# Inverse roots of the gating stage's norms: from ScalarE's tables to an integer step and three Newton steps on VectorE

## The chip, the cores and the metric

The kernel runs on one core of a Trainium2 chip. The metric is the device time of one execution in microseconds. The kernel before takes 2104.78 us, the median of three runs (2103.8 to 2104.8).

## The reference

One inference step of a two-layer encoder, for a prompt of 1024 rows and a sample of 32 rows that share weights, with 1024 channels. Layer 0 mixes by spatial gating, layer 1 by pooling; each layer has a squared-ReLU channel MLP of width 4096. RMS norms stand before and after each of them:

```python
def rmsnorm(x, g):
    y = x * lax.rsqrt(jnp.mean(x * x, axis=-1, keepdims=True) + EPS)
    return y * g

def sgu_mixer(h, w_in, g_v, w_s, b_s, w_out, T):
    z = jax.nn.gelu(h @ w_in)            # 1024 -> 4096
    u, v = jnp.split(z, 2, axis=-1)
    v = rmsnorm(v, g_v)                  # mean over 2048 values
    ...                                  # s = w_s v + b_s in chunks of 128 rows
    return (u * s) @ w_out, v

# trunk, one layer
x = x + gt1 * rmsnorm(mix, g_norm[i, 1])
h = rmsnorm(x, g_norm[i, 2]) * (1 + sc2) + sh2
f = jnp.square(jax.nn.relu(h @ ffn_w_up[i])) @ ffn_w_down[i]
x = x + gt2 * rmsnorm(f, g_norm[i, 3])
```

The change concerns how `lax.rsqrt` is computed for some of these norms.

## The kernel before

The 1056 rows are columns of three tiles: tile 0 and tile 1 have 384 prompt columns, tile 2 has 256 prompt and 32 sample columns. Channels lie on the partitions, in eight blocks (`KB`). Every product is made of three fp32r products: a matrix is split into a high and a low part (`wh`, `wl` for weights, `hh`, `hl` for inputs, `fh`, `fl` or `ush`, `usl` for hidden values). The high part is a copy on ScalarE (ACT), the low part a subtraction on VectorE (DVE); the matmuls run on TensorE (PE).

The gating layer goes through these stages. First the values `v` of all rows (the tile `pv`, `v_mm`, `v_end`): Gelu on ACT, a Square with accumulated sum, a store of `v`. `v_rms(t)` turns the sums of three row blocks into inverse roots `rv`, once per tile (L1283 on); the copies `wr` of the spatial weights are scaled with them. Then the items of `mixes`, two groups of 256 gate channels each: up products (`pu`), Gelu to `u`, the spatial product (`psp`), the gate, and the down products (`po`), whose sums lie in `acc`. Tile 0 goes first, then a pair stage for tiles 0 and 1 with combined inputs (`upairs`, `pgu`), then tile 2, then tiles 1 and 2. `sgu_stack.close()` ends the stage. After it come the MLP's up products `pf` and down products `pg`, first of tile 0, then of tile 1, then of both as a pair on combinations of the inputs (`combo`).

A norm over the channels is a `Stat`: ACT squares the blocks, DVE adds them, the sum is split (`sc` on ACT, `sm` on DVE), and two matmuls with ones (L977) give the sum `pn` in every partition. `Stat.finish` then takes the inverse root by `Abs_reciprocal_sqrt` on ACT (L981) and improves it by one Newton step: a Square on ACT (L982) and two scalar_tensor_tensors on DVE. `residual` multiplies by it and adds the old `x`, and starts the next `Stat`; `apply` makes `hh` and `hl` of the next product's input. In the profile the names carry the norm: `r_h` tile 2's input norm, `r_rs` the norm behind the gating, `r_r_0x` and `r_r_1x` the norms of tiles 0 and 1 in front of the MLP.

What an engine executes next is set in two steps. The program's own loop does it first: `weave` is called behind each product and pulls steps of the weight stream and of `fillers` (generators such as a tile's residual, or `u_sums`), as long as a planned DVE time is behind a planned PE time; `tick`, `tt`, `stt` and `ts` keep these times, and a filler that yields a number is not pulled again until the planned PE time has gone on by as much. Then the compiler's scheduler may still reorder. Each engine's queue is in order. A helper records every DVE operation, so these have one line, L80, in the profile. Weights come in through three raw buffers, with DMAs issued on SP.

`gelu` doesn't exist before the change; which norms run in the gating stage follows from the order of fillers: tile 2's input norm, tile 0's two norms behind the gating, and tile 1's first one.

Of the kernel before, what the change touches and what calls it, by code (L numbers as in the profile page):

```python
# [11 lines left out]
AF = mybir.ActivationFunctionType  # L12
ALU = mybir.AluOpType
# [3 lines left out]
D = 1024  # L17
# [18 lines left out]
def tile_stream_encoder_step(  # L36
# [25 lines left out]
    nc = tc.nc  # L62
    act = nc.scalar.activation
# [6 lines left out]
    def tick(us):  # L70
        time["pe"] += us
        time["dve"] = max(time["dve"], time["pe"] - 4.0)

    def on_dve(op, fixed, rate):
        def run(out, *args, **kw):
            n = 1
            for k in out.shape[1:]:
                n *= k
            time["dve"] += fixed + n / rate
            return op(out, *args, **kw)  # L80

        return run

    tt = on_dve(nc.vector.tensor_tensor, 0.07, 950.0)
    stt = on_dve(nc.vector.scalar_tensor_tensor, 0.13, 950.0)
    ts = on_dve(nc.vector.tensor_scalar, 0.13, 1900.0)
    turn32 = on_dve(nc.vector.transpose, 0.06, 880.0)

    def pool(name, **kw):
        return ctx.enter_context(tc.tile_pool(name=name, bufs=1, reuse_waits="tile", **kw))  # L90
# [15 lines left out]
    def acc_tile(t):  # L106
# [19 lines left out]
        out=quad, in_=ident.rearrange("p (c m) -> p m c", m=32), op=ALU.add, axis=AX.X  # L126
# [23 lines left out]
    def ps_ms(name):  # L150
        return psum.tile([P, 512], F32, tag="pm", bufs=3, name=name)

    def t_m(name):
        return work.tile([P, 384], F32, tag="m", bufs=3, name=name)
# [709 lines left out]
    def finish(tag):  # L864
        while any(f[0] == tag for f in fillers):
            pull(True)
        time["pe"] = max(time["pe"], time["dve"] - 3.0)


    def spread(t, ss, tag, out, dg):  # L870
# [18 lines left out]
        out.append(pb)  # L889
        yield False  # L890

    class Stat:


# [77 lines left out]
        def finish(self, out):  # L972
            n = self.n
            yield 1.2
            pn = ps_ms(f"pn_{self.tag}")
            for i, x in enumerate(self.parts):
                mm(pn[:, :n], onesr, x[:, :n], start=i == 0, stop=i == 1)  # L977
            tick(0.4)
            q = t_m(f"q_{self.tag}")[:, :n]
            r = work.tile([P, 384], F32, tag="rr", bufs=2, name=f"r_{self.tag}")[:, :n]  # L980
            act(out=r, in_=pn[:, :n], func=AF.Abs_reciprocal_sqrt, scale=1.0 / D)  # L981
            act(out=q, in_=r, func=AF.Square)  # L982
            yield 2.5
            stt(out=q, in0=pn[:, :n], scalar=-0.5 / D, in1=q, op0=ALU.mult, op1=ALU.mult)
            stt(out=r, in0=q, scalar=1.5, in1=r, op0=ALU.add, op1=ALU.mult)
            out.append(r)
            yield False


    def residual(st, l, cf, tag, out, store=True, stat=True, loads=None, r=None, small=False):  # L990
        t = st.t
        n = ncol[t]
        xos = {}

        def load(k2):
            xos[k2] = t_x(f"xo_{tag}_{k2}", [P, 2, n])
            i = nc.sync.dma_start(xos[k2], xd[t][:, 2 * k2 : 2 * k2 + 2, :])
            if loads is not None:
                loads.append(i.ins)

        if r is None:
            got = []
            yield from st.finish(got)
            r = got[0]
        st2 = Stat(t, tag + "x", small=small)
        for half in range(2):
            for k2 in (2 * half, 2 * half + 1):
                load(k2)
            for k2 in (2 * half, 2 * half + 1):
                for k in (2 * k2, 2 * k2 + 1):  # L1010
                    for c0, w, v in segs[t]:
                        a = A(t, k, c0, w)
                        stt(
                            out=a,
                            in0=a,
                            scalar=coef[:, l, cf, v, k : k + 1],
                            in1=r[:, c0 : c0 + w],
                            op0=ALU.mult,
                            op1=ALU.mult,
                        )  # L1020
                    yield True
                a = acc[t][:, 2 * k2 : 2 * k2 + 2, HALO:]
                tt(out=a, in0=a, in1=xos[k2], op=ALU.add)
                if stat:
                    st2.square(2 * k2, a)
                yield k2 % 2 == 0
        if store:
            nc.sync.dma_start(xd[t], acc[t][:, :, HALO:])
        out.append(st2)
# [253 lines left out]
    def v_rms(t):  # L1283
        c = slice(3 * t, 3 * t + 3)
        x, m, q = rv[:, c], rms[:, c, 0], rms[:, c, 1]
        nc.vector.tensor_reduce(out=x, in_=ssqv[:, c, :], op=ALU.add, axis=AX.X)
        ts(m, x, 1.0 / SGU, EPS, op0=ALU.mult, op1=ALU.add)
        act(out=x, in_=m, func=AF.Sqrt)
        nc.vector.reciprocal(out=x, in_=x)
        tt(out=q, in0=x, in1=x, op=ALU.mult)  # L1290
        stt(out=q, in0=q, scalar=-0.5, in1=m, op0=ALU.mult, op1=ALU.mult)
        stt(out=x, in0=q, scalar=1.5, in1=x, op0=ALU.add, op1=ALU.mult)

    hs = []

# [81 lines left out]
    for p, b in v_order:  # L1377
        ps = ps_dn(f"pv{p}_{b}")
        v_mm(ps, p, b, range(KB))
        v_end(ps, p, b)  # L1380
        next(h2_steps, None)
        if p == 2 and b < NT:
            with tc.issue_after(loads[("v", 2, 3)]):
                nc.sync.dma_start(xd[b], acc[b][:, :, HALO:])
        if p == 2 and b == NT - 1:
            u_open.append("acc")
        if p == 3 and b == 8:
            u_open.append("hs")
        if p == 3 and b % 3 == 2:
            v_rms(b // 3)  # L1390
        weave()
# [290 lines left out]
    def pair_item(p, after, ends, gate=None):  # L1682
# [59 lines left out]
        def up(jp):  # L1742
# [10 lines left out]
            if jp == 0:  # L1753
                flush()
                finish("combos" if gate is None else "usums")
                if state["kept"]:
                    state["kept"] = 0
                    for i in range(2):
                        x = w_tile(f"fu{i}", ("fu", i))
                        u_places.append((x[:, :n], x[:, n : 2 * n]))  # L1760
# [64 lines left out]
        if passes[p + 1][2] != PAIR:  # L1825
            slack[0] = 0.0
            finish(f"ffn{l}_{NT - 1}")
            fillers.append(late_norm.pop())
# [170 lines left out]
    for p, (gs, tiles) in enumerate(mixes):  # L1999
# [3 lines left out]
        for t in tiles:  # L2003
            sgu_item(p, t, mix, to_ffn0 if gs[-1] == 7 and t > 0 else None)

    sgu_stack.close()
    late = pool("late")

# [165 lines left out]
    def run_ffn(l, after):  # L2174
        for p, (pl, c, tiles, m) in enumerate(passes):
            if pl != l:
                continue
            ends = [t for t in tiles if not any(q[0] == l and t in q[2] for q in passes[p + 1 :])]
            if tiles == PAIR:
                pair_item(p, after, ends)  # L2180
                continue
            for t in tiles:
                if c == 0:
                    if any(f[0] == f"ffn{l}_{t}" for f in fillers):
                        flush()
                    finish(f"ffn{l}_{t}")
                ffn_item(p, t, after if t in ends else None)
# [158 lines left out]
```

## Time and profile before

| | us |
|---|---|
| median of three runs | 2104.78 |
| the profiled execution | 2107.3 |
| its span | 2105.5 |
| PE busy | 2078.7 |
| DVE busy | 1637.3 |
| ACT busy | 1069.1 |

The span is from the first instruction of the program to the last one; the profiled execution has 1.8 us around it. Rows of a timeline give the start in us, the duration in us, engine, line, operation, out<-in by the program's names, shapes, how many were merged, and in brackets the idle time of the engine just before and what ended it. ACT_TABLE_LOAD is ScalarE's change of its table of functions. The page says of itself that matmuls are pipelined and that their ends are modelled.

### The profile page before, as it was taken

How to read it: one execution, taken by the hardware profiler on the slowest of the kernel's cores; microseconds unless marked ns; L12 is line 12 of the kernel's file. 1: busy time of each engine (PE TensorE's matmuls, PEld its weight loads, DVE VectorE, ACT ScalarE, POOL GpSimd, SP SyncE). 2: the span in 40 equal slices, each digit the busy share in tenths (PEclk: the TensorE clock that was granted, in tenths of full speed). 3: DMA queues.
4: the chain of work that ended last, by engine and by line, in shares of the span. 5: the costliest groups of instructions: out<-in, count | busy, mean ns of one | idle time of the engine just before them, and what ended most of it. 6: DMA issues, size and time to landing. Idle time of an engine off the chain costs nothing.

```text
span 2105.5 us, 32900 instructions
## 1 busy us (share of the span) xinstructions
PE 2078.7 (99%) x12742; PEld 2003.3 (95%) x12742; DVE 1637.3 (78%) x2935; ACT 1069.1 (51%) x1911; POOL 22.3 (1%) x44
## 2 busy tenths in 40 slices
PE   8999999999999999999999999999999999999998
PEld 6877999999999999999999999999999999999998
DVE  6799676889799988887767989897868654579554
ACT  5634543454246643344436766776435443365555
POOL 0000000000000000000000000000000000001100
PEclk9999999999999999999999999999999999999999
DMA  8585543365445443443334767643323321148863
GB/s 295 164 263 180 183 118 112 119 192 189 140 126 150 123 133 112 129 120 121 111 91 130 215 194 237 187 148 108 92 76 106 90 81 52 51 125 235 202 181 93
DMA packets 410738, 303.91 MB, mean 144 GB/s; under 512 B 47022, under 2 KB 373974, under 8 KB 410580
## 3 DMA queue, kind: packets, MB, share of 16 engines
q1 hardware_dynamic: 409652, 300.52, 47.7%
q8 instruction: 100, 1.64, 0.3%
q0 software_dynamic: 896, 1.28, 0.2%
q14 instruction: 58, 0.48, 0.1%
q10 hardware_dynamic: 32, 0.01, 0.0%
HBM read 271.09 MB, written 30.66 MB: 143 GB/s over the span
## 4 chain that ended last, share of the span: by engine, by line
PE 81%; DVE 10%; DMA 5%; ACT 3%; issue 2%; SPq 0%; DVEq 0%; ACTq 0%
PE pg L1105 11%; PE pg L1104 11%; PE pg L1106 11%; PE pf L1104 4%; PE pf L1106 4%; PE pf L1105 4%; PE pfa L1728 3%; PE pfa L1730 3%; PE pfa L1729 3%; DVE aa L80 2%; DMA raw<-in_w_ada_dram 2%; PE po L1104 2%; PE po L1105 2%; PE po L1106 2%; PE pfb L1728 1%
## 5 line engine op out<-in xcount | busy, mean ns | idle before, releaser
L1104 PE MATMUL pg<-fh,wh_dn 128*128 128x384 f32 (+1 forms) x960 | 311.4, 324 | 0.2 <-DVE acc L80 0.2
L1105 PE MATMUL pg<-fl,wh_dn 128*128 128x384 f32 (+1 forms) x960 | 310.1, 323 | 0.0
L1106 PE MATMUL pg<-fh,wl_dn 128*128 128x384 f32 (+1 forms) x960 | 309.6, 323 | 0.0
L80 DVE TENSOR_TENSOR acc<-acc,pg 128x384 f32<-128x384 f32 (+1 forms) x272 | 144.4, 532 | 110.4 <-PE pg L1106 109.1
L80 DVE TENSOR_TENSOR wl_dn<-raw,wh_dn 128x1024 fp32r<-128x1024 f32 x136 | 166.1, 1222 | 68.9 <-ACT wh_dn L580 36.1
L80 DVE SCALAR_TENSOR_TENSOR aa<-raw,csil,aa 128x512 f32<-128x512 f32 (+1 forms) x364 | 208.2, 622 | 13.5 <-DMA raw<-in_w_ada_dram 13.2
L1104 PE MATMUL pf<-hh,wh_up 128*128 128x288 f32 (+1 forms) x632 | 192.5, 305 | 0.0
L1105 PE MATMUL pf<-hl,wh_up 128*128 128x288 f32 (+1 forms) x632 | 191.1, 302 | 0.0
L1106 PE MATMUL pf<-hh,wl_up 128*128 128x288 f32 (+1 forms) x632 | 190.8, 302 | 0.0
L580 ACT ACTIVATE wh_dn<-raw 128x1024 fp32r<-128x1024 f32 x136 | 143.9, 1058 | 91.5 <-PE pf L1105 32.8
L1104 PEld LDWEIGHTS pg<-fh,wh_dn 128*128 128x128 f32 x960 | 180.2, 188 | 1.4 <-ACT fh L1424 0.6
L1105 PEld LDWEIGHTS pg<-fl,wh_dn 128*128 128x128 f32 x960 | 180.2, 188 | 0.6 <-DVE fl L80 0.2
L1106 PEld LDWEIGHTS pg<-fh,wl_dn 128*128 128x128 f32 x960 | 180.1, 188 | 0.0
L580 ACT ACTIVATE wh_up<-raw 128x1024 fp32r<-128x1024 f32 x79 | 83.7, 1059 | 82.5 <-PE pg L1105 45.8
L80 DVE TENSOR_TENSOR wl_up<-raw,wh_up 128x1024 fp32r<-128x1024 f32 x79 | 96.4, 1220 | 29.9 <-ACT wh_up L580 29.5
L1106 PEld LDWEIGHTS pf<-hh,wl_up 128*128 128x128 f32 x632 | 118.9, 188 | 0.3 <-DVE wl_up L80 0.3
L1105 PEld LDWEIGHTS pf<-hl,wh_up 128*128 128x128 f32 x632 | 118.6, 188 | 0.4
L1104 PEld LDWEIGHTS pf<-hh,wh_up 128*128 128x128 f32 x632 | 118.5, 187 | 0.6 <-ACT wh_up L580 0.2
L80 DVE TENSOR_TENSOR wl_up_S<-raw,wh_up_S 128x512 fp32r<-128x512 f32 (+1 forms) x84 | 71.8, 866 | 55.7 <-PE pfb L1729 45.7
L1104 PE MATMUL pg<-fx,wh_dn 128*128 128x288 f32 (+1 forms) x352 | 109.2, 311 | 0.2 <-ACT fx L1424 0.2
L1105 PE MATMUL pg<-fx,wh_dn 128*128 128x288 f32 (+1 forms) x352 | 108.3, 308 | 0.0
L1106 PE MATMUL pg<-fx,wl_dn 128*128 128x288 f32 (+1 forms) x352 | 108.0, 307 | 0.0
(827 smaller groups left out, 5651.1 us busy)
## 6 DMA issues: line engine op xcount, KB each, us to landing
raw<-in_ffn_w_up_dram SPq DMA_DIRECT2D x136, 512.0 KB, 4.1
raw<-in_ffn_w_down_dram SPq DMA_DIRECT2D x136, 512.0 KB, 4.0
raw<-in_w_ada_dram SPq DMA_DIRECT2D x90, 512.0 KB, 4.6
raw<-in_sgu_w_in_dram SPq DMA_DIRECT2D x48, 512.0 KB, 4.7
raw<-in_sgu_w_out_dram SPq DMA_DIRECT2D x32, 512.0 KB, 3.9
xd<-acc SPq DMA_DIRECT2D x8, 1536.0 KB, 8.2
xo_r<-xd SPq DMA_DIRECT2D x32, 384.0 KB, 4.5
vd<-vt SPq DMA_DIRECT2D x32, 256.0 KB, 4.1
```

What stands on the lines that cost most here:

```text
L80: return op(out, *args, **kw)
L580: act(out=wh, in_=r, func=AF.Copy)
L1104: mm(ps[:, :n], wh, rh, start=i == 0, stop=False)
L1105: mm(ps[:, :n], wh, rl, start=False, stop=False)
L1106: mm(ps[:, :n], wl, rh, start=False, stop=i == last)
L1728: mm(ps[:, :n], wh[:, o], rh, start=first and k == 0, stop=False, skip_group_check=True)
L1729: mm(ps[:, :n], wh[:, o], rl, start=False, stop=False, skip_group_check=True)
L1730: mm(ps[:, :n], wl[:, o], rh, start=False, stop=k == HK - 1, skip_group_check=True)
```

## The change

`v_rms` takes its inverse root without ACT: the bits of the mean square, read as an integer, are multiplied by -0.5 and added to a constant, which gives the bits of a first guess; three Newton steps on DVE follow. `Stat.finish` does the same while the flag `gelu[0]` is set, which is until `sgu_stack.close()`; there the Square of each step stays on ACT, and each added step yields 1.5 us of planned time. Behind the stage the old way is kept.

```diff
+    HALF_EXPONENT, I32 = 1597463007.0, mybir.dt.int32
...
         def finish(self, out):
...
-            act(out=r, in_=pn[:, :n], func=AF.Abs_reciprocal_sqrt, scale=1.0 / D)
+            if gelu[0]:
+                ts(r.bitcast(I32), pn[:, :n].bitcast(I32), -0.5, HALF_EXPONENT + 5 * 2.0**23, op0=ALU.mult, op1=ALU.add)
+                for _ in range(2):
+                    act(out=q, in_=r, func=AF.Square)
+                    yield 1.5
+                    stt(out=q, in0=pn[:, :n], scalar=-0.5 / D, in1=q, op0=ALU.mult, op1=ALU.mult)
+                    stt(out=r, in0=q, scalar=1.5, in1=r, op0=ALU.add, op1=ALU.mult)
+            else:
+                act(out=r, in_=pn[:, :n], func=AF.Abs_reciprocal_sqrt, scale=1.0 / D)
             act(out=q, in_=r, func=AF.Square)
             yield 2.5
             stt(out=q, in0=pn[:, :n], scalar=-0.5 / D, in1=q, op0=ALU.mult, op1=ALU.mult)
             stt(out=r, in0=q, scalar=1.5, in1=r, op0=ALU.add, op1=ALU.mult)
...
+    gelu = [True]
...
     def v_rms(t):
...
-        act(out=x, in_=m, func=AF.Sqrt)
-        nc.vector.reciprocal(out=x, in_=x)
-        tt(out=q, in0=x, in1=x, op=ALU.mult)
-        stt(out=q, in0=q, scalar=-0.5, in1=m, op0=ALU.mult, op1=ALU.mult)
-        stt(out=x, in0=q, scalar=1.5, in1=x, op0=ALU.add, op1=ALU.mult)
+        ts(x.bitcast(I32), m.bitcast(I32), -0.5, HALF_EXPONENT, op0=ALU.mult, op1=ALU.add)
+        for _ in range(3):
+            tt(out=q, in0=x, in1=x, op=ALU.mult)
+            stt(out=q, in0=q, scalar=-0.5, in1=m, op0=ALU.mult, op1=ALU.mult)
+            stt(out=x, in0=q, scalar=1.5, in1=x, op0=ALU.add, op1=ALU.mult)
...
+    gelu[0] = False
     sgu_stack.close()
```

## The prediction

> **What bounds the kernel now.** I read the page first (busy times and the chain that ended last), then TensorE's waits, then the timelines of PE, ACT and DVE around each wait that stands near a removed instruction.
>
> ```profile
> span 2105.5 us, 32900 instructions
> PE 2078.7 (99%) x12742; PEld 2003.3 (95%) x12742; DVE 1637.3 (78%) x2935; ACT 1069.1 (51%) x1911; POOL 22.3 (1%) x44
> PE 81%; DVE 10%; DMA 5%; ACT 3%; issue 2%; SPq 0%; DVEq 0%; ACTq 0%
> ```
>
> TensorE is busy 2078.7 of 2105.5 us, so all its idle time is 26.8 us, most of it at the start and in stages that the change doesn't touch. The change leaves every matmul in place. It can only remove or add TensorE waits, and only where the new code runs: from the values' stage to the first up products, 80 to 660 us. 0.2% of the run, about what a measurement of this kernel can tell from no change, is 4.2 us. The waits there that end on ACT or DVE are few:
>
> ```profile
> PE pgu L1104 <- DVE acc L80: 1.2, 1, 1.2
> PE pu L1104 <- ACT u L1570: 1.1, 2, 0.6
> PE po L1104 <- ACT acc L1430: 1.1, 1, 1.1
> PE pn_r_0x L977 <- ACT sc_r_0x L930: 0.9, 1, 0.9
> PE po L1105 <- DVE usl L80: 0.6, 1, 0.6
> ```
>
> The columns are who waited for whom, us in total, times, longest. The first of them is outside the changed code. One of the two on u has a removed load in front of it (below).
>
> ```profile
> 440.00:500.00 60.00, 56.70 (x417) 55.26 (x416) 49.40 (x97) 36.55 (x56) 0.62 (x2) 1.00 0.73 228
> 500.00:575.00 75.00, 75.00 (x514) 74.65 (x513) 61.89 (x120) 21.93 (x33) 0.94 (x3) 1.00 0.46 142
> 616.00:660.00 44.00, 44.00 (x277) 43.68 (x277) 43.23 (x73) 31.89 (x58) 0.00 (x0) 1.00 0.53 159
> ```
>
> These stages (length; busy us of PE, PEld, DVE, ACT, POOL; clock; DMA) show the room for more VectorE work: 10.6 us of idle DVE from 440 to 500, 13.1 us from 500 to 575, and only 0.8 us from 616 to 660. The granted clock is 1.00 throughout.
>
> **Part 1: table loads that go.** The Sqrt of the values' norm (L1288) and the reciprocal root of the other norms (L981) each change ScalarE's table, and the next Gelu (L1142, L1570) changes it back:
>
> ```profile
> L1288 ACT ACT_TABLE_LOAD  x3: 1283/1283/1283, 193.0 to 230.3; - x3
> L981 ACT ACT_TABLE_LOAD  x4: 1283/1283/1283, 78.9 to 616.4; - x4
> L1142 ACT ACT_TABLE_LOAD  x3: 1283/1283/1283, 81.2 to 211.6; - x3
> L1570 ACT ACT_TABLE_LOAD  x3: 1283/1283/1283, 231.8 to 506.0; - x3
> ```
>
> That is 13 loads. In the compiled order of the changed kernel one remains, before the first root that still uses the table (tile 1's second norm): 12 x 1.283 = 15.4 us less ScalarE time. ScalarE is half idle, so only loads in front of a waiting matmul count.
>
> Place A, the last values' norm, with the PE row that waited for u:
>
> ```profile
> 230.29 1.28 ACT L1288 ACT_TABLE_LOAD   x1
> 231.81 1.28 ACT L1570 ACT_TABLE_LOAD   x1
> 233.11 0.87 ACT L1570 ACTIVATE u<-pu 128x384 f32<-128x384 f32 x2
> 233.65 0.44 PE L1104 MATMUL pu<-hh,wh_u 128*128 128x384 f32 x1 [0.62 <-ACT u L1570]
> ```
>
> Without the two loads and the small root between them u starts 2.8 us earlier, at 230.3; the wait of 0.62 us goes whole. What is next late is nothing on PE. **-0.6 us.**
>
> Place B, tile 0's first norm:
>
> ```profile
> 458.83 1.28 ACT L981 ACT_TABLE_LOAD   x1
> 460.12 0.49 ACT L981 ACTIVATE r_rs<-pn_rs 128x384 f32<-128x384 f32 x1
> 460.63 1.28 ACT L1570 ACT_TABLE_LOAD   x1
> 463.10 0.40 PE L1104 MATMUL po<-ush,wh_o 128*128 128x288 f32 x1 [1.11 <-ACT acc L1430]
> ```
>
> The copy that frees the PSUM bank stands behind both loads. In the changed order it stands first, and three Squares are spread between the following copies. **-1.1 us.** The loads of the values' stage (79 to 83, 193 to 213 us) have no PE wait behind them: 0.
>
> [...] From 458.83 to the next activation at 460.12 a load took 1.29 us. [...]
>
> **Part 2: VectorE work that comes.** Each of the norms that run with the flag set (tile 2's input norm, tile 0's two, tile 1's first) gains one tensor_scalar and two rounds of two scalar_tensor_tensors on DVE and of one Square on ACT. The present round shows the price:
>
> ```profile
> 462.78 0.56 DVE L80 SCALAR_TENSOR_TENSOR q_rs<-pn_rs,q_rs 128x384 f32<-128x384 f32 x1 [2.17 <-ACT q_rs L982]
> 463.37 0.56 DVE L80 SCALAR_TENSOR_TENSOR r_rs<-q_rs,r_rs 128x384 f32<-128x384 f32 x1
> ```
>
> Five of 0.56 are 2.8 us per norm, 11 us in all. The integer step has no row; below it lies half such an instruction, above it a whole one, and I take the whole one since it reads PSUM as the first row does. The values' norm goes from 6 small DVE instructions to 12. One lasts 0.16 us, 0.2 with its wait for the one before:
>
> ```profile
> 232.04 0.16 DVE L80 TENSOR_TENSOR mod<-rv 128x3 f32<-128x3 f32 x1
> ```
>
> 6 x 0.2 = 1.2 us each, 3.6 us for three. At place A they stand between the three multiplications that psp needs, which had 1.5 us to spare. Cost on PE 0; if that cover were gone, at most 1.2 us.
>
> The chain of a norm becomes longer by two trips DVE-ACT-DVE, 3 to 5 us with the steps held apart by the yields. For tile 2:
>
> ```profile
> 95.58 0.64 DVE L80 SCALAR_TENSOR_TENSOR hl<-mt,mod,hh 128x256 fp32r<-128x256 f32 x2
> 96.36 0.60 ACT L1142 ACTIVATE vt<-pv 128x512 f32<-128x512 f32 x1 [0.80 <-PE pv L1132]
> 101.93 0.60 ACT L1142 ACTIVATE vt<-pv 128x512 f32<-128x512 f32 x1 [4.22 <-PE pv L1132]
> ```
>
> Its last part was ready at 96.2. PE began the first block that reads it at 96.4 and ended that at 101.9, using one of eight parts each 0.7 us, so the last is due at 101.2. Some 3 us later, less the two loads' 2.6 us that stood in the old chain, it stays ahead: 0. For tile 0 the input is wanted only at 600 us. In between the longer chain changes the order: the split sum's matmul, which waited at place C, now stands 96 matmuls (13 us) later, behind the next item's products, while its inputs come about 5 us later:
>
> ```profile
> 480.09 0.45 PE L977 MATMUL pn_r_0x<-sc_r_0x,ones 128*128 128x384 f32 x1 [0.87 <-ACT sc_r_0x L930]
> 490.11 1.22 DVE L80 TENSOR_TENSOR wl_u<-raw,wh_u 128x1024 fp32r<-128x1024 f32 x1
> 491.75 0.40 PE L1105 MATMUL po<-usl,wh_o 128*128 128x288 f32 x1 [0.63 <-DVE usl L80]
> ```
>
> **Place C: -0.9 us.** At place D usl stood behind a 1.22 us weight split on DVE. In the new order a 0.28 us copy and a 0.6 us multiplication stand there: **-0.3 us** (0 to -0.6). On SP three weight loads now go ahead of the 1.5 MB store of tile 0, which helps D if anything. The 5.6 us that DVE gains in 440 to 575 fit its idle 23.7 us; where aa work is dense just after 500 I allow **+0.3 us** (0 to 1).
>
> **Part 3: the load that remains, and the full stage.** From 616 to 660 DVE has 0.8 us idle and tile 1's first norm brings 2.8.
>
> ```profile
> 643.89 0.61 DVE L80 SCALAR_TENSOR_TENSOR sm_r_1x<-sq_r_1x,eps,sc_r_1x 128x384 fp32r<-128x384 f32 x1
> 646.75 1.22 DVE L80 TENSOR_TENSOR wl_up<-raw,wh_up 128x1024 fp32r<-128x1024 f32 x1
> 645.60 0.34 PE L977 MATMUL pn_r_1x<-sc_r_1x,ones 128*128 128x384 f32 x1
> 647.33 0.53 ACT L1634 ACTIVATE r<-r 128x384 f32<-128x384 f32 x1
> 648.16 0.52 ACT L1424 ACTIVATE fh<-r 128x384 fp32r<-128x384 f32 x1
> 648.74 0.44 PE L1104 MATMUL pg<-fh,wh_dn 128*128 128x384 f32 x1
> 661.17 1.14 DVE L80 SCALAR_TENSOR_TENSOR hl<-acc,mod,hh 128x384 fp32r<-128x384 f32 x2
> 663.07 0.33 PE L1104 MATMUL pf<-hh,wh_up 128*128 128x384 f32 x1
> ```
>
> In the new order DVE has ahead of sm_r_1x, besides what it had: the five Newton instructions (2.5 us; two queued ones of this size, hl, take 1.14 together, a pitch of 0.5), one fl (0.5), one wl_up (1.1), combo_y and combo_z (0.9 each, three quarters of the wl_up row by size), 5.9 us. sm ends at 644.5 + 5.9 = 650.4, combo_z just before it starts, 649.8. PE goes through 18 instructions from pn to the first product of the last fh, 645.60 to 648.74, 0.174 us each; now 27 down products stand ahead of pn, so it reaches pn's second half at 645.6 + 30 x 0.174 = 650.8 and doesn't wait for DVE. But ACT's order is now: combo_R (which waits for combo_z), Square, the table load, r_r_1x, fh. From 649.8: 0.5 + 0.4 + 1.3 + 0.4 + 0.5 = 652.9. PE's next instruction behind pn is the product of that fh, due at 651.0, with nothing in between; before, 14 products stood there. A wait of 1.9 us and a restart of 0.2: **+2.1 us** at place E. The removed load of 616 was hidden; the one that takes its place is not. Bounds: 0.5 if DVE finds idle time, 4 if the three trips each hold DVE about 0.7 us.
>
> Tile 1's hl then ends some 5 to 7 us later. Its last block was ready at 662.3, and used 7 blocks of 3 products behind 663.07, at 666.7; PE is 2 us later too, and the new order puts four products more ahead of it: 0, at most 1.
>
> **Sum:** -0.6 - 1.1 - 0.9 - 0.3 + 0.3 + 2.1 = -0.5 us. The profiled execution took 2107.3 us, span 2105.5 and 1.8 around it; it becomes 2106.8. The three timed runs have the median 2104.78, 2.5 us below it, so the forecast is **2104.3 us**.
>
> **Rivals.** (1) Slower: the ping-pong of DVE and ACT in the full stage. With in-order queues a Newton step on DVE waits for a Square that stands on ACT behind a Relu and its Square; three trips at about 1 us, then the load behind a late combo_z, give E 5 to 6 us and the following up products 1. With the gains of A to D (2.9) halved, since usl and acc queue behind the same waits at 460 to 490: about +5, 2110 us. It decides once E passes 4 us plus whatever gains are left. For it speaks the 43.23 of 44 us; against it, that wl_up_A, needed at 682 us, has the same sum of DVE work ahead of it as before. Chance 0.15.
> (2) Faster: DVE's stage catches up in the idle time before 616, fh is not late, D goes whole (0.8), and the weights that come ahead of the store also take away the wait of pgu on acc (1.2): -0.6 - 1.1 - 0.9 - 0.8 - 1.2 = -4.6, 2100.2 us. Against it: DVE's order from 245 to 455 us doesn't change. Chance 0.11.
> (3) The waits at A to D only move, because the chain there runs through weight loads (DMA 5%, DVE 10% of it): gains 0, E stays, +2.1: 2106.9 us. Chance 0.2.
> (4) The loads don't go: excluded by the compiled order.
>
> **Numbers.** The forecast's own case has 0.54, from 2102 to 2107. Faster by over 0.2% 0.11, slower 0.15, the rest 0.74. The range goes from just beyond rival 2 to short of rival 1's end: 2099.8 to 2109.2.
>
> **What would show it.** Right: one of the 13 table loads left; no PE wait on u near 233, on acc near 462, on sc near 480; a new wait of about 2 us on ACT fh near 650, right behind pn_r_1x, with a table load just ahead of r_r_1x. Wrong: a PE wait on hh or hl of tile 1 near 664, on hh or hl of tile 2 near 96, or E outside 0.5 to 4 us.

## The result, and the profile after

The changed kernel takes 2108.29 us, the median of 22 runs (2106.06 to 2110.65), beside 2104.84 us for the kernel before: a ratio of 1.0015 with the 95% interval [1.0009, 1.0020], some 3.2 us slower. Forecast were 2104.3 us, a gain of 0.5. The time lies inside the range and the loss is below 0.2%, but it is a loss that this many runs can tell from no change, and the forecast had the other sign. The profiled execution took 2110.65 us, 1.8 of it around the span.

The page of the changed kernel, busy times and the chain that ended last:

```profile
span 2108.9 us, 32925 instructions
PE 2080.2 (99%) x12742; PEld 2006.9 (95%) x12742; DVE 1648.6 (78%) x2973; ACT 1057.5 (50%) x1900; POOL 22.4 (1%) x44
PE 85%; DVE 7%; DMA 3%; ACT 3%; issue 1%; SPq 0%; DVEq 0%; ACTq 0%
```

DVE has 11.3 us more, ACT 11.6 us less, and the chain runs through PE even more than before. PE's busy time grew by 1.5 us with the same 12742 matmuls. So some matmuls took longer, though the change leaves every matmul in place.

TensorE's waits (who for whom, us in total, times, longest):

```profile
PE pg L1116 <- ACT fh L1436: 2.2, 1, 2.2
PE pfa L1740 <- ACT a L1746: 1.9, 3, 1.3
PE psp L1513 <- DVE wr L80: 1.5, 2, 1.1
```

Of the waits that the prediction listed, those on acc (place B), on sc_r_0x (place C) and on usl at 491 us (place D) are gone, and so is the one on u near 233 (place A). In their place the first row shows the forecast wait on fh, and the third one a wait on wr that was not forecast; a wait of 0.9 us on usl near 456 us is new too in this profile.

ScalarE around place E, in the changed kernel:

```profile
648.58 0.62 ACT L932 ACTIVATE sc_r_1x<-sq_r_1x,eps 128x384 fp32r<-128x384 f32 x1 [2.86 <-DVE sq_r_1x L80]
649.48 0.51 ACT L1928 ACTIVATE combo_R<-combo_z 128x384 fp32r<-128x384 f32 x1
649.89 0.51 ACT L1646 ACTIVATE r<-r 128x384 f32<-128x384 f32 x1
650.42 1.28 ACT L991 ACT_TABLE_LOAD   x1
651.71 0.49 ACT L991 ACTIVATE r_r_1x<-pn_r_1x 128x384 f32<-128x384 f32 x1
652.10 0.51 ACT L1436 ACTIVATE fh<-r 128x384 fp32r<-128x384 f32 x1
```

TensorE at the same place:

```profile
649.25 0.44 PE L979 MATMUL pn_r_1x<-sc_r_1x,ones 128*128 128x384 f32 x1 [0.51 <-ACT sc_r_1x L932]
650.00 0.44 PE L979 MATMUL pn_r_1x<-sm_r_1x,ones 128*128 128x384 f32 x1
652.67 0.79 PE L1116 MATMUL pg<-fh,wh_dn 128*128 128x384 f32 x3 [2.23 <-ACT fh L1436]
653.56 0.53 PE L1118 MATMUL pg<-fh,wl_dn 128*128 128x384 f32 x1
653.88 0.53 PE L1117 MATMUL pg<-fl,wh_dn 128*128 128x384 f32 x1
...
656.44 0.53 PE L1117 MATMUL pg<-fl,wh_dn 128*128 128x384 f32 x1
656.76 0.41 PE L1118 MATMUL pg<-fh,wl_dn 128*128 128x384 f32 x1
```

The order on ACT is the forecast one: combo_R, Square, table load, root, fh, end at 652.6. PE waits 2.23 us for it. Two things are new. PE had already waited 0.51 us for sc_r_1x, which stands on ACT behind a late sum of squares. And behind the wait the products start 0.32 us apart, from 653.56 to 656.76, where 0.173 is the usual pitch. The windows of the changed kernel say the same by the granted clock (length; busy us of PE, PEld, DVE, ACT, POOL; clock; DMA):

```profile
653.00:657.00 4.00, 4.00 (x15) 3.88 (x14) 3.52 (x7) 3.47 (x9) 0.00 (x0) 0.57 0.02 7
657.00:660.00 3.00, 3.00 (x19) 3.00 (x19) 2.39 (x5) 2.15 (x4) 0.00 (x0) 1.00 0.47 156
```

At 0.57 of the clock, 15 matmuls pass in 4 us where 23 would. In the trace of the kernel before the granted clock stays at 1.00 from 9 to 2100 us.

A count of the matmuls that PE starts from 600 to 660 us makes a yardstick for place E; those that a version lacks at its end are 384 wide. First the kernel before, then the changed one:

```profile
600.00:660.00 60.00, 60.00 (x395) 59.68 (x394) 54.93 (x100) 38.79 (x70) 0.00 (x0) 1.00 0.52 155
```

```profile
600.00:660.00 60.00, 57.22 (x367) 56.30 (x366) 50.81 (x94) 35.11 (x62) 0.00 (x0) 0.97 0.46 140
```

28 fewer at 0.173 us are 4.8 us. A second measure agrees: both traces hold 12742 matmuls, and by the start of the n-th one in each, the changed kernel is 2.0 us ahead at 640 us of the kernel before and 3.1 us behind at 655, a loss of 5.0. The same view over the values' stage, before and after, is the gain's side:

```profile
150.00:250.00 100.00, 99.26 (x488) 82.56 (x487) 82.27 (x203) 49.27 (x85) 0.00 (x0) 1.00 0.61 187
```

```profile
150.00:250.00 100.00, 100.00 (x500) 84.84 (x499) 79.69 (x211) 39.31 (x71) 0.00 (x0) 1.00 0.61 191
```

Twelve more at 0.173 us are some 2 us gained there; by the n-th matmul it is 1.9 us. Only 0.9 of it lies at place A. The other 1.0 is gained at 175 to 180 us, between the removed loads at 79 to 83 and those from 193 us on. There the kernel before has the weight copies wh_v on ScalarE between combinations, and the products come late three times, as at 175.87, 0.43 us behind the one ahead in place of 0.23:

```profile
173.52 1.04 ACT L580 ACTIVATE wh_v<-raw 128x1024 fp32r<-128x1024 f32 x1
174.47 0.51 ACT L1334 ACTIVATE combo_acc<-usum_z 128x384 fp32r<-128x384 f32 x1
175.44 0.39 PE L1130 MATMUL pv<-wh_v,hh 128*128 128x512 f32 x1
175.87 0.50 PE L1131 MATMUL pv<-wl_v,hh 128*128 128x512 f32 x1
```

In the changed kernel three such copies stand together, and the products don't come late:

```profile
171.31 2.95 ACT L580 ACTIVATE wh_v<-raw 128x1024 fp32r<-128x1024 f32 x3
```

All twelve profiles that hold the new values' norm have this gain, so it goes with the new order of the instructions; no run tests that order alone.

### The profile page after: what moved, and what is told of

It is laid out like the page before. It is cut to its first block, busy times and chain, and to the rows that moved or that the text cites. A ratio compares the mean times of both kernels' runs of the same rounds, so it can differ in the third digit from the quotient of the medians.

```text
span 2108.9 us, 32925 instructions
## 1 busy us (share of the span) xinstructions
PE 2080.2 (99%) x12742; PEld 2006.9 (95%) x12742; DVE 1648.6 (78%) x2973; ACT 1057.5 (50%) x1900; POOL 22.4 (1%) x44
## 4 chain that ended last, share of the span: by engine, by line
PE 85%; DVE 7%; DMA 3%; ACT 3%; issue 1%; SPq 0%; DVEq 0%; ACTq 0%
PE pg L1117 11%; PE pg L1116 11%; PE pg L1118 11%; PE pf L1116 4%; PE pf L1117 4%; PE pf L1118 4%; PE pfa L1740 3%; PE pfa L1742 2%; PE pfa L1741 2%; PE pv L1142 2%; PE pv L1144 2%; PE pv L1143 2%; PE po L1116 2%; PE po L1118 2%; PE po L1117 2%; PE pu L1116 2%
```

## The experiments

Theory 1 is the prediction's own place E with a larger price: the table load that is left, now in front of fh, and VectorE's later chain make a wait at 650 us, and the wait brings a stretch at half pace behind it. Its rivals: VectorE's chain alone, wherever the load stands; the norms of tile 0, by the new waits near 480 us; the planned spacing of the added rounds. Each time stands beside runs of the kernel before on the same chip.

**Tile 1's first norm back to the root.** This puts the load back to 613 us and takes five instructions from VectorE.

```diff
-            if gelu[0]:
+            if gelu[0] and self.tag != "rs_1":
```

> Changed kernel, but tile 1's first norm takes the ScalarE root again: its table load is back near 616 us, five instructions of 0.56 us are gone from VectorE between 616 and 625. Theory 1 (all of the loss lies at 650): no wait on fh near 650, no stretch at half pace there, about -5.5 us against the changed kernel, 2103, which is also below the kernel before (gains A to C stay). Rival (the new waits near 455 and 480 us, from the other norms, make the loss): 2107 to 2108.

Measured 2104.10 us beside 2105.76 of the kernel before, ratio 0.9991 [0.9982, 0.9999]. The load stands in the work of ACT where PE doesn't wait for it, fh comes at 644.78, and the count is that of the kernel before:

```profile
600.00:660.00 60.00, 60.00 (x395) 59.68 (x394) 55.12 (x98) 39.73 (x71) 0.00 (x0) 1.00 0.51 151
```

So the loss at 600 to 660 us hangs wholly on this one norm. What the rest of the change does is a small gain at most, since the interval ends at 0.9999.

**The load alone taken out of the way.** Tile 1's first norm stays with Newton; one tiny activation behind it brings the table.

```diff
             stt(out=r, in0=q, scalar=1.5, in1=r, op0=ALU.add, op1=ALU.mult)
+            if self.tag == "rs_1":
+                act(out=junk1, in_=r[:, 0:1], func=AF.Abs_reciprocal_sqrt)
             out.append(r)
```

> Changed kernel, with one activation on a single column added at the end of tile 1's first norm (near 624 us) that brings the root's table; the load thus leaves its place ahead of fh near 650, and nothing else moves. Theory 1 (the loss is the load in front of fh at 650, enlarged by the half pace of the products behind that wait): the wait of 2.2 us on fh falls to about 0.9, the 0.32 us pitch of the 13 products behind it goes back to 0.173, together -1.3 - 1.8: about 2105 us. Theory 2 (the load's place does not matter, VectorE's longer chain makes the wait): the wait stays above 2 us, 2108. Theory 3 (the half pace does not hang on the length of the wait): -1.3 alone, 2107.

Measured 2106.75 us, ratio 1.0003 [0.9995, 1.0012]. TensorE and its windows in this kernel:

```profile
648.01 0.44 PE L979 MATMUL pn_r_1x<-sc_r_1x,ones 128*128 128x384 f32 x1 [0.50 <-ACT sc_r_1x L932]
650.19 0.80 PE L1118 MATMUL pg<-fh,wh_dn 128*128 128x384 f32 x3 [0.99 <-ACT fh L1438]
```

```profile
600.00:660.00 60.00, 58.47 (x382) 57.33 (x381) 53.03 (x95) 38.01 (x69) 0.00 (x0) 1.00 0.48 146
```

The wait fell by 1.24 us, just about the load, and the half pace went with it: 15 matmuls more than in the changed kernel, 2.6 us. That is theory 1 for the wait, but not for the time, which lies above its 2105: 13 matmuls are still missing against the kernel before, 2.2 us. They go once the added Newton work goes, as the run before this one shows. Taken away in this order, load and Newton chain share the loss nearly evenly. Behind the 2.23 us that both together give the wait there is a stretch at half pace, behind 0.99 us there is none, and no run has the load in front of fh without the Newton work, so what the load alone would cost is not shown.

**More Newton.** The two following norms lose the root as well, so the load moves on to tile 2.

```diff
-            if gelu[0]:
+            if gelu[0] or self.tag in ("r1_0_1x", "rs_2"):
```

> Changed kernel, and the two norms behind tile 1's first (tile 1's second, tile 2's first) also go by the integer step and Newton, so the last table load moves from 650 to some 767 us, and VectorE gets 2.8 + 2.3 us more between 650 and 665. Theory 1 (the load makes the wait): the wait on fh at 650 falls by 1.3 + 0.4 and the half pace behind it goes; but hl of tile 1 comes some 4 us later, near 670, which may cost up to 3 us: 2104 to 2107. Theory 2 (VectorE's chain makes the loss): worse than the changed kernel, 2109 to 2112.

Measured 2107.57 us, ratio 1.0010 [1.0001, 1.0019], just above the upper end of theory 1 and below theory 2. The wait on fh is 0.83 us without half pace, but hl of tile 1 is now late:

```profile
666.35 0.44 PE L1117 MATMUL pf<-hl,wh_up 128*128 128x384 f32 x1 [0.53 <-DVE hl L80]
```

The load's part goes, and more VectorE work in a stage without idle VectorE time gives part of that back.

**Tile 0's norms back to the root.**

```diff
-            if gelu[0]:
+            if gelu[0] and self.tag not in ("rs_0", "r1_0_0x"):
```

> Changed kernel, but tile 0's two norms take the ScalarE root again, with their table loads at 459 and 495 us. Theory 1: the stretch 600 to 750 us stays as in the changed kernel; in 440 to 500 the waits of the kernel before come back (1.1 on acc, 0.9 on sc_r_0x, 0.6 on usl) and those near 455 (0.9 on usl) and 480 us (1.1 on wr, 0.5 on u, then 3 us at half pace) go: about even, 2107.5 to 2109. Rival (the norms of tile 0 make the loss by the half pace near 483): 2105.

Measured 2109.69 us, ratio 1.0018 [1.0009, 1.0027]: as slow as the changed kernel, though the new waits near 480 us are gone and the old one on sc_r_0x is back. From 600 to 660 us it starts 368 matmuls, one more than the changed kernel. The rival that blames tile 0's norms falls.

**The planned spacing.**

```diff
-                    yield 1.5
+                    yield 0.0
```

> Changed kernel with a planned pause of 0 in place of 1.5 us in the two added rounds, so the instructions of a norm stand closer together in the order. If the planned spacing made the chain late at 650: the wait of 0.5 us on sc_r_1x goes, and that on fh falls below 1.5, 2105.5. If VectorE's work and the load make it, whatever the spacing: 0.5 and 2.2 us stay and the time is that of the changed kernel, 2108.

Measured 2109.91 us, ratio 1.0018 [1.0009, 1.0027]. The spacing is not the cause. Two combo_R now stand ahead of sc_r_1x on ACT, PE waits 1.49 us for sc and 2.04 for fh, and 358 matmuls start from 600 to 660 us, the fewest of all.

**The changed kernel again, and the first version again.**

> The changed kernel once more, beside the two others of this call. Theory 1: the wait of 2.2 us on fh near 650 and some 13 products at half pace behind it stand in this profile too, since they follow from the order of the instructions; the stretch at half pace near 483, behind waits of 1.1 and 0.5 us, need not, since waits of 1.4 to 1.9 us at the same place in other versions had none. Ratio to the kernel before 1.0015.

> The version in which tile 1's first norm keeps the ScalarE root, once more: ratio to the kernel before 0.9991, and to the changed kernel beside it 0.9976 (5 us), if the loss is at 650 us and the gains before 500 us are real; 1.000 to the kernel before if those gains were chance.

Measured 2108.53 us, ratio 1.0014 [1.0005, 1.0022], and 2104.17 us, ratio 0.9992 [0.9983, 1.0001]. Their medians are 4.4 us apart, close to the 4.8 us counted at place E. The wait of 2.22 us and the half pace at 650 come again in the changed kernel's second profile:

```profile
650.32 0.80 PE L1116 MATMUL pg<-fh,wh_dn 128*128 128x384 f32 x3 [2.22 <-ACT fh L1436]
652.02 0.53 PE L1118 MATMUL pg<-fh,wl_dn 128*128 128x384 f32 x1
```

Near 480 us its waits are 0.82 on wr and 0.99 on u, and the clock behind them stays at 1.00. In the first profile 1.10 and 0.53 us were followed by 3 us at a clock of 0.50. The windows of the first and then of the second profile:

```profile
483.00:486.00 3.00, 3.00 (x10) 3.00 (x11) 3.00 (x7) 1.05 (x3) 0.00 (x0) 0.50 0.91 276
```

```profile
482.00:486.00 4.00, 3.90 (x22) 3.91 (x23) 3.82 (x10) 1.24 (x4) 0.00 (x0) 1.00 0.83 234
```

So the half pace at that place comes and goes, the one at 650 stays.

**The values' norm alone.** Everything else as before.

```diff
-            if gelu[0]:
-                ...
-            else:
-                act(out=r, in_=pn[:, :n], func=AF.Abs_reciprocal_sqrt, scale=1.0 / D)
+            act(out=r, in_=pn[:, :n], func=AF.Abs_reciprocal_sqrt, scale=1.0 / D)
```

> The change in the values' norm alone; the other norms are as in the kernel before. By the prediction's step A the wait of 0.6 us on u near 233 goes, nothing else: 2105.2 against 2105.8 of the kernel before (ratio 0.9997). By the sum of PE's delays in the changed kernel's trace from 150 to 250 us (1.4 against 3.3 us) it would be -1.9: ratio 0.9991.

Measured 2104.66 us beside 2105.64, ratio 0.9996 [0.9988, 1.0005]. The interval holds both expectations. The trace starts 497 matmuls from 150 to 250 us, nine more than before, which speaks for the larger one; the timed runs don't decide. Since 1.0 us of this lies at 175 to 180 us, step A alone is 0.8 here.

**One Newton round fewer.** In the version with tile 1's first norm by the root:

```diff
-                for _ in range(2):
+                for _ in range(1):
```

> As the version in which tile 1's first norm keeps the ScalarE root, and in the Newton norms that remain (tile 2's input, tile 0's two) one of the three rounds is left out, so the roots are rougher: two instructions of 0.56 us and one trip DVE-ACT-DVE less for each. If the waits near 455 and 480 us come from VectorE's longer chain: the 1.4 us on wr at 479 shrinks to 0.5 or less, ratio to the kernel before 0.9985. If they come from the order in which the weight loads arrive: the waits stay, ratio 0.9991 as before.

Measured 2104.89 us, ratio 0.9997 [0.9988, 1.0006]. The wait on wr doesn't shrink, it is 1.91 us here. VectorE's timeline of this kernel shows why:

```profile
478.36 1.22 DVE L80 TENSOR_TENSOR wl_u<-raw,wh_u 128x1024 fp32r<-128x1024 f32 x1
479.50 0.28 DVE L1468 COPY wt<-wsT 128x128 f32<-128x128 f32 x1
480.98 0.46 DVE L80 TENSOR_TENSOR usl<-s,ush 128x288 fp32r<-128x288 f32 x1 [1.20 <-ACT ush L1436]
481.51 0.11 DVE L1469 MEMSET wt<- 64x64 f32 x1
481.65 1.23 DVE L80 TENSOR_TENSOR wl_u<-raw,wh_u 128x1024 fp32r<-128x1024 f32 x1
482.79 0.63 DVE L80 TENSOR_SCALAR wr<-wt,rv 128x128 f32<-128x128 f32 x3
```

wr stands behind a usl that waits for ACT and behind a weight split. That is the order in the queue, not the length of a norm's chain.

**A wait without a table load.** To see whether the load or the wait brings the half pace, the load is early as above, and a plain activation of 1536 columns (3072 in a second kernel) stands in front of fh:

```diff
+                if self.tag == "r1_0_1x":
+                    act(out=self.sq[:, 4:8, :], in_=self.sq[:, 0:4, :], func=AF.Square, bias=self.parts[1].bitcast(F32)[:, 0:1])
                 act(out=r, in_=pn[:, :n], func=AF.Abs_reciprocal_sqrt, scale=1.0 / D)
```

> The early load (as in the run that brought the root's table at 624 us), and in front of fh near 650 stands one activation of 1536 columns instead, about 1.5 us long, whose result nobody uses: the wait of the changed kernel without its table load. If the length of the wait decides on the half pace: a wait of about 2.1 us on fh and, as in the changed kernel, some 13 products behind it 0.32 us apart, granted clock near 0.6 there. If the table load itself brought it: a wait of 2.1 us and products 0.173 us apart from the fourth on.

> The same with 3072 columns, about 2.8 us: a wait of some 3.5 us. If the half pace lasts for a fixed time once a wait is long enough: again some 13 products 0.32 us apart (about 4 us). If it grows with the wait: 20 or more.

One run each, of 2109.00 and 2109.74 us. Windows of the first, cut where the clock changes, with a wait on fh of 1.88 us that ended at 650.89:

```profile
648.90:652.31 3.41, 1.53 (x9) 1.30 (x9) 1.15 (x3) 3.41 (x8) 0.00 (x0) 1.00 0.75 209
652.31:655.73 3.42, 3.42 (x12) 3.35 (x12) 3.42 (x7) 2.45 (x5) 0.00 (x0) 0.50 0.01 2
```

And of the second, with a wait of 3.16 us that ended at 651.93:

```profile
648.76:652.17 3.41, 0.25 (x2) 0.19 (x1) 0.40 (x2) 3.41 (x4) 0.00 (x0) 1.00 0.71 199
652.17:655.58 3.41, 3.32 (x11) 3.06 (x11) 2.87 (x7) 3.29 (x9) 0.00 (x0) 0.50 0.00 0
```

With no load there, the half pace comes all the same, so it belongs to the wait. It lasts 3.41 us behind either wait and doesn't grow with it. It begins 1.4 us after PE has started again in the one and 0.2 us after it in the other, at nearly the same time in both; the last section shows the steps that it keeps to.

## Why the prediction was wrong, point by point

**Places A to D.** The four waits went as forecast. A itself came out at 0.9 us in place of 0.6. The values' stage as a whole gained 1.6 to 2 us by the counts, 9 to 12 matmuls more: the 1.0 us at 175 to 180 was in no term of the prediction, which counted the stage at nothing outside A. B's 1.1 us is an upper end, since the runs that keep the load at 459 us had 0.1 (tile 0 by the root) and 0.5 us (values alone) at that place. The 0.9 us of C and the 0.6 of D (0.3 in the sum) became little or no gain: waits on wr and u at 479 to 482 us took their place, 1.5 to 1.8 us in the second profiles of the two repeated kernels. Rival 3 (the waits only move) holds for these two places alone.

**Place E, the step that failed.** The wait on fh came near its size: 2.23 us and a restart of 0.27 against 1.9 and 0.2. Two terms were missing. PE was held to wait nowhere ahead of fh; but only sm, the second half of the split sum, was followed, and the first half's sc waits for the same late sum of squares: 0.51 us and a restart of some 0.15. And a wait was priced at its own length: the half pace behind it costs the difference of 0.32 and 0.173 us for 11 or so products, 1.6 us. Together 0.51 + 0.15 + 2.23 + 0.27 + 1.6 = 4.8 us, the number that the count gives, beyond the bound of 4. The prediction took its prices from waits of at most 1.2 us, and behind those the kernel before shows no slow stretch.

That the wait on fh came so near is in part luck, for VectorE's chain was later than forecast:

```profile
620.53 0.56 DVE L80 SCALAR_TENSOR_TENSOR q_rs<-pn_rs,q_rs 128x384 f32<-128x384 f32 x1 [1.05 <-ACT q_rs L986]
648.46 0.96 DVE L80 TENSOR_TENSOR combo_z<-combo_y,combo_x 128x768 f32<-128x768 f32 x1
```

combo_z ends at 649.42. The forecast's 649.8, less the 2.0 us that the changed kernel is ahead by then, is 647.8, so the chain is 1.6 us late; VectorE's waits for the Squares of the added rounds, 1.05 and 0.23 us, are most of that. PE came later to fh as well, since sc and sm had held it, and so the wait on fh alone shows little of the delay.

**Part 2.** The integer step took 0.56 us, as taken. The two waits on tile 1's and tile 2's hh and hl stayed away. VectorE was to get some 11 and 3.6 us more work and got 11.3 in all. In the full stage the chain's cost was called hidden but for E; in the order of the runs VectorE's part of E is 2.2 us and the load's, with the half pace, 2.6. The load that remains takes 1.29 us to the next activation (650.42 to 651.71), as at 458.83 before.

**The rivals.** Rival 1's price of 5 to 6 us for E and its sign come nearest. Its mechanism, three trips of about 1 us between DVE and ACT, shows in part: one wait of 1.05 us on q_rs and one of 0.23; the spacing run shows that closing these trips up doesn't help. Its deciding point for a loss over 0.2%, E above 4 us plus the gains left, so some 6 us, was not passed by 4.8, and the loss is 0.15%. Rival 2 didn't come; its sum counts D at 0.8 where the row has 0.63.

**What stays open.** Gains of about 2 (the values' stage with A), 0.1 to 1.1 (B), none for C and D, less 4.8 to 5.0 at E, leave a loss of 1.7 to 2.9 us where the timed runs show 3.2 (1.9 to 4.2 by the interval). Waits on a at 700 to 725 us, from none to 1.9 us from run to run (0.6 before), are too uneven to tell. The version with tile 1's first norm by the root beats the changed kernel by 4.4 us; against the kernel before its gain of some 1.6 us touches the limit of what the runs can tell, with 0.9991 [0.9982, 0.9999] and 0.9992 [0.9983, 1.0001].

## What to carry to other kernels

When table loads are taken out one by one, look at where the last one comes to stand and not at their number alone: twelve fewer went with gains of 2.1 to 3.1 us in this case, and the one that moved from a covered place to the front of a waiting matmul took 2.6 us, with the half pace behind it. So let the last user of the other table keep its place, or try a tiny activation that brings the table early, which took back 2.6 of 4.8 us here. And where both halves of a split feed PE, follow both back: the first half made PE wait 0.51 us in the changed kernel. The wait of 2.23 us on fh cost 4.1 us with its restart (0.27) and the half pace behind it (1.6), nearly twice its length.

## What the runs showed of the hardware

Behind the wait of 2.23 us in the changed kernel, which has the table load in front of fh, and behind those of 1.88 and 3.16 us, which have a plain activation there, the granted clock is 0.50 for 3.41 us. In the spacing run the mean clock from 600 to 660 us is 0.94 where the changed kernel has 0.97, so an estimate from these two means (the missing share of 60 us, over 0.5) gives 7.2 us at half pace in place of 3.6; PE waits there twice, 1.49 us on sc up to 648.54 and 2.04 us on fh up to 651.68. In the first profile of the changed kernel the two slow stretches before the end start a whole number of steps of 3.413 us apart: 482.83 and 653.50 are 50 steps. The windows of the steps ahead of them and of the stretches themselves:

```profile
479.42:482.83 3.41, 1.86 (x15) 1.49 (x13) 3.30 (x8) 1.33 (x3) 0.00 (x0) 1.00 0.93 286
482.83:486.24 3.41, 3.33 (x10) 3.33 (x11) 3.41 (x9) 1.22 (x4) 0.00 (x0) 0.50 0.89 265
650.08:653.50 3.42, 1.19 (x5) 0.82 (x6) 1.35 (x3) 3.39 (x7) 0.00 (x0) 1.00 0.81 222
653.50:656.91 3.41, 3.41 (x12) 3.41 (x12) 2.93 (x6) 2.88 (x7) 0.00 (x0) 0.50 0.01 4
```

So in these profiles the idle time of PE counted in such steps tells more than the length of a wait. The kernel with one Newton round fewer has two single waits of nearly the same length, 1.91 us on wr that ended at 483.13 and 1.9 on a in the step from 717.58. The first falls into two steps, and the clock stays; the second lies in one, and the step behind it is at half:

```profile
478.65:482.06 3.41, 2.57 (x20) 2.31 (x18) 2.11 (x5) 1.69 (x3) 0.00 (x0) 1.00 0.91 266
482.06:485.47 3.41, 2.34 (x18) 2.34 (x18) 3.41 (x8) 1.90 (x2) 0.31 (x1) 1.00 0.71 237
717.58:720.99 3.41, 1.49 (x9) 1.17 (x8) 2.96 (x5) 1.44 (x2) 0.00 (x0) 1.00 0.57 164
720.99:724.40 3.41, 3.41 (x13) 3.41 (x12) 2.19 (x4) 0.52 (x1) 0.00 (x0) 0.50 0.72 236
```

The changed kernel's waits near 480 us fit this. In the first profile 1.10 and 0.53 us lie nearly whole in one step, from 479.42, which has 1.55 us of idle time, and the half pace follows. In the second profile 0.82 and 0.99 us brought none; the mean clock of 0.88 from 651 to 652 us puts the start of its slow stretch at 651.76 by an estimate, and 50 steps ahead of that, at 481.1, a step ends between the two waits.

Among the steps shown here and those behind 400 us in the traces of the kernel before and of the changed kernel, each of the four in which PE is idle for 1.88 us or more (1.88, 1.92, 2.23, 3.16) is followed by one at half, and so is the one with 1.55; none with 1.31 or less is (1.31 from 708.11 in the changed kernel, 1.20 from 411.40 in the kernel before). These few steps don't tell how much idle time it takes, and the cause in the chip is not shown, only this count.
